# Three moves in the order of VectorE's work: differences of the first set, a left-over product, and the gates' low parts in a hybrid decoder layer

## The chip, the cores and the metric

The kernel runs on one core of a Trainium2 chip. The metric is the device time of one execution in microseconds (us); the kernel before takes 1325.04 us in the median of three runs (1324.93 to 1326.69). Engines are named as in the profile: PE is TensorE's matmuls and PEld its weight loads, DVE is VectorE, ACT is ScalarE, POOL is GpSimd, SP is SyncE, which here issues nearly all DMAs.

## The reference

One decoder layer on 2048 tokens of width 1024, in float32. Cut to what matters:

```python
xn = rms_norm(h, ln_g)
b_gate, c_gate, x_conv, g_conv, x_lru, g_lru = split(xn @ w_in)      # 6 x 1024 columns
y_conv = b_gate * causal_conv3(c_gate * x_conv)                      # group A
u = causal_conv4(x_lru) + conv_b                                     # group B
r = sigmoid(u_per_head @ w_a + b_a); i = sigmoid(u_per_head @ w_i + b_i)
a = exp(8 * r * log_sigmoid(lam))
h_t = a_t * h_(t-1) + sqrt(1 - a_t**2) * (i_t * u_t)                 # scan over the tokens
y = concat(headwise_rms(y_conv) * silu(g_conv), headwise_rms(h) * silu(g_lru))
out = rms_norm(h + y @ w_out)
```

Nearly all arithmetic lies in the two projections, 2048 x 1024 x 6144 and 2048 x 2048 x 1024. The gates r and i are small matmuls, 64 x 64 for each of 16 heads.

## The kernel before

**Precision.** Every float32 operand of a matmul is split into a high part (a cast to fp32r on ACT) and a low part (the value less its high part, a subtraction, mostly on DVE, in the helper at line 163). A product of two split operands is three matmuls: high x high, high x low, low x high. In the profile th and tl are the parts of the moving operand (the tokens' side), s holds both parts of the weights, st both parts of the gates' operand.

**Seven products instead of eight.** A projection step computes two column blocks of 128 for 1024 tokens as a 2 x 2 block product by the Strassen-Winograd scheme: seven products, numbered 0 to 6, on sums and differences of the four blocks of each operand. A product is four blocks of 128 of the inner dimension (j = 0 to 3) times three matmuls, so 12 matmuls into one PSUM accumulator of 128 x 512 (`bank`, five buffers in the pool of the products, two in that of the gates). Products share accumulators: 0, 1 and 2 and 5 go into A, 3 and 6 into B, 4 into C. After product 0 ACT copies A out to q1, after product 1 to u2, after product 2 to rr (lines 1299, 1302, 1305); the next product into A must wait for that copy. The helper `put` then combines accumulators and copies into the four results 11, 12, 21, 22 on DVE.

**Steps, slots, order.** There are 64 steps. Steps 0 to 23 are the input projection of the first 1024 tokens, in rounds of three: l (group B's x and gate), a (c and x of group A), b (its b and gate). Steps 24 to 47 do the same for the second 1024 tokens, 48 to 55 and 56 to 63 the output projection. A step runs its products slot by slot in program order, and the order of all engines' instructions is the program's own (the scheduler is told to keep it). Work behind a product is put off by slots: `at(n, f)` runs f at the n-th following `tick()`, and each slot begins with a tick, which runs what is due in the order in which it was put there. Each engine works its instructions strictly in this order, so an instruction that waits holds up all that stand behind it.

Usually slot 0 runs product 0, slot 1 the sixth product that the step before left over (`pend`: it goes into that step's B), and slots 2 to 6 the products 1, 3, 2, 4, 5; the step's own product 6 is left over again (`ORDER`, lines 1245 to 1318). When the set of tokens or the projection changes, the moving operands change too. The opening step (24, 48, 56) runs eight plain products, and the step after it (25, 49, 57, called late) the order `AFTER`, 0, 4, 5, 1, 3, 2, and leaves product 6 over to the next.

**The first three steps** have no sums and differences of the tokens' blocks yet. They run eight plain half products each, in eight slots (`plain`, lines 1166 to 1177). In their shadow the differences are made: `bit(j)` (line 1140) lists four pieces of work for each j, with six subtractions on DVE and two casts on ACT for each j: b12 - b11 and b22 - b12, then b22 less the first, with the casts and low parts of the operands 2 and 1, and the raw value of operand 6 (`last`). `do_bits(n)` runs the next n of these 16 pieces. The second step (step 1) runs two in each of its eight slots (`after1`), so all of them; the third step (`after2`) casts operands 3 and 6, prepares the weights of step 3 with `prep`, and calls `do_bits(2)` too, which finds nothing left.

**The tokens' change.** Class `Change` makes the operands of the second set, its method `of_x(q)` slot by slot: q is 0 to 7 in step 23, 8 to 15 in step 24, 16 to 21 in step 25. Operand 6 is the last. At q = 21, slot 5 of step 25, `sixth(0, 1)` subtracts, casts and takes the low parts for j = 0 and 1; a tick later, in slot 0 of step 26, `sixth(2, 3)` does so for j = 2 and 3. Slot 1 of step 26 runs the left-over product of step 25, which reads operand 6.

**The gates.** In an l step, `lru` (lines 693 to 799) puts off its work after result 12: the convolution u, then `sth`, which casts u's halves of 64 partitions into the two tiles st[0] and st[1]; a slot later `stl`, two subtractions of 64 x 1024 on DVE for the low parts; two slots on `gates(0)`, four matmuls on the first 512 tokens, two on st[0] and two on st[1] (line 736), then `sigs(0)`, four sigmoids on ACT (line 743) that free the two PSUM buffers; and, two slots after gates(0), `gates(1)` and `sigs(1)` for the other 512 tokens.

Of the kernel before, what the change touches and what calls it, by code (L numbers as in the profile page):

```python
# [12 lines left out]
F32 = mybir.dt.float32  # L13
F32R = mybir.dt.float32r
AF = mybir.ActivationFunctionType
ALU = mybir.AluOpType
# [4 lines left out]
C = 512  # L21
NC = S // C
NB = C // P
# [15 lines left out]
def hymba_kernel(ctx: ExitStack, tc: tile.TileContext, x, xt, w_in, par, lamc, w_gate, w_out, final_g, out):  # L39
# [27 lines left out]
    def piece(name):  # L67
        return rawp.tile([P, C], F32, tag="raw", name=name)
# [75 lines left out]
    def at(slots, *fs):  # L144
        if slots == 0:
            for f in fs:
                f()
        else:
            due.append([slots, fs])
# [12 lines left out]
    def tt(out, a, b, op, eng=None):  # L162
        (eng or nc.vector).tensor_tensor(out=out, in0=a, in1=b, op=op)  # L163
# [99 lines left out]
    def set_of(n):  # L263
        kind, h, _ = steps[n]
        return h + (2 if kind == "o" else 0)

    def opens(n):
        return n > 0 and set_of(n) != set_of(n - 1)
# [153 lines left out]
    class Change:  # L422
# [34 lines left out]
            for i, v in ((2, b11), (3, b12), (1, b22), (6, b21)):  # L457
                self.r[i, j] = v

        def sixth(self, *js):  # L460
            for j in js:
                tt(self.r[6, j], self.r[6, j], self.r[1, j], ALU.subtract)
            self.cut([(6, j) for j in js])

        def of_x(self, q):
            if q == -4:
                for j in range(NB):
                    self.get(5, j, piece("traw"))
            if q == 0:
                self.pair(0)  # L470
                self.pair(1)
            if q == 3:
                for j in range(NB):
                    self.get(4, j, piece("traw"))
                self.pair(2)
                self.pair(3)
            if 9 <= q <= 12:
                self.sums(q - 9)
            if q == 21:
                self.sixth(0, 1)  # L480
                at(1, lambda: self.sixth(2, 3))
            self.cut({1: ((5, 0), (5, 1)), 2: ((5, 2), (5, 3)), 4: ((0, 0), (0, 1)), 5: ((4, 0), (4, 1)),
                      6: ((4, 2), (4, 3)), 7: ((0, 2), (0, 3)), 8: ((7, 0), (7, 1)), 9: ((7, 2), (7, 3)),
                      11: ((1, 0),), 12: ((1, 1),), 13: ((1, 2), (1, 3)), 14: ((3, 0), (3, 1)),
                      17: ((3, 2), (3, 3)), 18: ((2, 0), (2, 1)), 19: ((2, 2), (2, 3))}.get(q, ()))
# [205 lines left out]
    LO, HI = slice(0, 64), slice(64, P)  # L691
    N2 = 2 * C

    def lru(h, k, late=0, early=0):
# [6 lines left out]
        v = {}  # L701
# [20 lines left out]

        def stl():
            st = v["st"]
            for j, (hi, lo) in enumerate(((LO, HI), (HI, LO))):
                tt(st[j][lo], v["u"][hi], st[j][hi].bitcast(F32), ALU.subtract)

        def gates(i):
            sl = slice(i * C, (i + 1) * C)
# [308 lines left out]
    with tc.manual_schedule(engines={ENG.PE, ENG.Activation, ENG.DVE, ENG.Pool, ENG.SP}):  # L1038
# [122 lines left out]
        def do_bits(n):  # L1161
            for f in bits[:n]:
                f()
            del bits[:n]
# [14 lines left out]
        def after1(s):  # L1179
            i = {2: 2, 3: 3, 5: 0, 7: 1}.get(s)  # L1180
            if i is not None:
                s_hi(2, i)
            do_bits(2)
            if i is not None:
                s_lo(2, i)

# [9 lines left out]
        load_next(3)  # L1196

        def after2(s):
            do_bits(2)
            if s in (1, 2, 3, 4, 6, 7):  # L1200
                prep(3, (0, 1, 2, 3, 0, 4, 5)[s - 1])
            if s >= 4:
                j = s - 4
                for i, v in ((3, tr[j][1]), (6, t6[j])):
                    T[i, j] = t_tile(i, j)
                    nc.scalar.copy(T[i, j][0], v)
                for i, v in ((3, tr[j][1]), (6, t6[j])):
                    low(v, T[i, j])
# [7 lines left out]
        for n in range(PLAIN, N):  # L1216
            kind, h, k = steps[n]
            S_ = Sn[n]
            last = n + 1 == N
            new = not last and set_of(n + 1) != set_of(n)  # L1220
            soon = n + 2 < N and set_of(n + 2) != set_of(n + 1)
            put = lru(h, k, 2) if opens(n) and kind == "l" else consumer[kind](h, k)
            if n == 3 * KT + 6:
                work_on[0] = jobs()
            if opens(n):
                cc = {}
                for s, (which, i, t) in enumerate(((12, 1, 5), (22, 3, 5), (11, 1, 4), (21, 3, 4),
                                                   (11, 0, 0), (12, 0, 7), (22, 2, 7), (21, 2, 0))):
                    tick()
                    change.slot(8 + s)  # L1230
                    if s in (0, 3, 4, 6):
                        prep(n + 1, (3, 4, 5, 6)[(0, 3, 4, 6).index(s)])
                    first = which not in cc
                    if first:
                        cc[which] = bank()
                    for j in range(NB):
                        mm(cc[which], S_, T, i, j, first and j == 0, not first and j == NB - 1, k=t)
                    if not first:
                        put(which, cc[which], None)
                    if s == 4:  # L1240
                        load_next(n + 2, 4)
                continue
            late = opens(n - 1)
            bk = {}
            slots = (0, 6) + ORDER[1:] if not late else AFTER
            for s in range(6 if late else 8 if new or last else 7):
                i = slots[s]
                place[0] = {"l": 0, "a": 7, "b": 14}.get(kind, 0) + s
                tick()
                if soon and s == 3:  # L1250
                    T2 = {}
                    change = Change(set_of(n + 2), T2)
                if soon and s > 3:
                    change.slot(s - 8)
                if new:
                    change.slot(s)
                if late:
                    change.slot(16 + s)
                    if s == 0:
                        prep(n, 7)  # L1260
                elif n > 0 and opens(n - 2):
                    if s == 0:
                        prep(n, 5)
                        prep(n, 6)
                    elif s == 2:
                        prep(n, 7)
                elif s == 0:
                    prep(n, 6)
                elif s == 2:
                    prep(n, 7)  # L1270
                if new and s > 0:
                    if s in (1, 3, 4, 5):
                        prep(n + 1, (1, 3, 4, 5).index(s) + 1)
                    elif s > 5:
                        prep(n + 2, s - 5)
                elif s > 0:
                    prep(n + 1, s - 1)
                if s == 3:
                    load_next(n + 2, 3 if late else 4)
                if s == 1 and not late:  # L1280
                    if pend is not None:
                        S6, B, put0, u20 = pend
                        alone = B is None
                        if alone:
                            B = bank()
                        for j in range(NB):
                            mm(B, S6, T, 6, j, alone and j == 0, j == NB - 1, not alone)
                        put0(21, B, u20)
                        pend = None
                    continue  # L1290
                b = {0: "A", 1: "A", 2: "A", 5: "D" if late else "A", 3: "B", 6: "B", 4: "C"}[i]
                first = b not in bk
                if first:
                    bk[b] = bank()
                for j in range(NB):
                    mm(bk[b], S_, T, i, j, first and j == 0, j == NB - 1, not first)
                if i == 0:
                    q1 = sm_q1[0] = sm("q1")
                    nc.scalar.copy(q1, bk["A"])  # L1299
                elif i == 1:  # L1300
                    u2 = sm_u2[0] = sm(("u2", "rr")[n % 2])
                    nc.scalar.copy(u2, bk["A"])  # L1302
                elif i == 2:
                    rr = sm(("rr", "u2")[n % 2])
                    nc.scalar.copy(rr, bk["A"])
                    put(22, bk["B"], rr)
                    if late:
                        put(12, bk["D"], rr)
                elif i == 4:
                    put(11, bk["C"], q1)  # L1310
                elif i == 5 and not late:
                    put(12, bk["A"], None)
                elif i == 6:
                    put(21, bk["B"], u2)
            if new:
                T = T2
            elif not last:
                pend = (S_, bk["B"], put, u2)
# [46 lines left out]
```

## Time and profile before

| what | value |
|---|---|
| median of three runs | 1325.04 us (1324.93 to 1326.69) |
| profiled execution, its own time | 1325.2 us |
| its span in the profile | 1323.4 us |
| mean granted clock of TensorE | 0.997 |
| busy: PE, PEld, DVE, ACT, POOL | 1293.5, 1058.0, 1040.3, 749.1, 245.2 us |
| data moved by DMA | 355.29 MB, 268 GB/s over the span |

The span is the profiled part of that execution, from the first instruction to the last; the time includes what lies around it. A timeline row gives start, duration, engine, line, operation, output<-inputs, shapes and count; the brackets give the idle time of the engine before the row and what ended it. A row of the waits gives the waiting engine and line, who ended the wait, the total in us, how often, and the longest. Matmuls are pipelined: one is shown with about 0.39 us, and the next starts 0.23 us after it. A row with x2 or x3 merges instructions that follow one another, and its duration runs from the first start to the last end. The line 163 is the helper of all two-operand operations, so these are told apart by their tiles.

### The profile page before, as it was taken

How to read it: one execution, taken by the hardware profiler on the slowest of the kernel's cores; microseconds unless marked ns; L12 is line 12 of the kernel's file. 1: busy time of each engine (PE TensorE's matmuls, PEld its weight loads, DVE VectorE, ACT ScalarE, POOL GpSimd, SP SyncE). 2: the span in 40 equal slices, each digit the busy share in tenths (PEclk: the TensorE clock that was granted, in tenths of full speed). 3: DMA queues.
4: the chain of work that ended last, by engine and by line, in shares of the span. 5: the costliest groups of instructions: out<-in, count | busy, mean ns of one | idle time of the engine just before them, and what ended most of it. 6: DMA issues, size and time to landing. Idle time of an engine off the chain costs nothing.

```text
span 1323.4 us, 16676 instructions
## 1 busy us (share of the span) xinstructions
PE 1293.5 (98%) x5688; PEld 1058.0 (80%) x5688; DVE 1040.3 (79%) x1252; ACT 749.1 (57%) x1141; POOL 245.2 (19%) x189
## 2 busy tenths in 40 slices
PE   7989999999999999999999999999999999999997
PEld 6868878787878787878888888888888788887886
DVE  7789898999989897978566676667549777649886
ACT  7576758566675657466554545364457433445453
POOL 3204233344334340002010110101011000000000
PEclk9999999999999999999999999999999999999999
DMA  7138787888989888542789999999779887697654
GB/s 292 32 116 292 279 288 251 299 327 277 339 289 324 294 295 300 195 157 74 247 314 297 333 354 332 338 350 363 237 273 330 267 257 239 235 404 276 231 181 160
DMA packets 157958, 355.29 MB, mean 268 GB/s; under 512 B 16944, under 2 KB 51760, under 8 KB 157872
## 3 DMA queue, kind: packets, MB, share of 16 engines
q1 hardware_dynamic: 153264, 338.17, 73.7%
q0 software_dynamic: 4320, 15.73, 3.1%
q8 instruction: 45, 0.74, 0.2%
q14 instruction: 41, 0.34, 0.1%
q10 hardware_dynamic: 288, 0.32, 0.1%
HBM read 217.11 MB, written 137.04 MB: 268 GB/s over the span
## 4 chain that ended last, share of the span: by engine, by line
PE 55%; DVE 22%; DMA 10%; issue 6%; ACT 6%; SPq 1%; POOL 0%; DVEq 0%; ACTq 0%; POOLq 0%
PE bank L999 53%; DVE s L163 5%; DVE tl L163 2%; DVE u L710 2%; DMA s<-so 2%; PE gate L736 2%; DMA sd<-s 1%; DVE st L163 1%; DVE r L770 1%; DMA raw<-in_w_in_dram 1%; DMA xr<-od 1%; DVE sums L641 1%; DVE traw L163 1%; ACT i L743 1%; ACT r L743 1%
## 5 line engine op out<-in xcount | busy, mean ns | idle before, releaser
L999 PE MATMUL bank<-th,s 128*128 128x512 f32 x3632 | 1130.2, 390 | 9.6 <-ACT rr L1302 2.8
L999 PEld LDWEIGHTS bank<-th,s 128*128 128x128 f32 x3632 | 682.1, 188 | 157.4 <-ACT rr L1302 4.1
L999 PE MATMUL bank<-tl,s 128*128 128x512 f32 x1816 | 707.8, 390 | 1.8 <-DVE tl L163 1.6
L999 PEld LDWEIGHTS bank<-tl,s 128*128 128x128 f32 x1816 | 341.1, 188 | 75.0 <-DVE tl L163 3.4
L163 POOL TENSOR_TENSOR s<-raw,s 128x512 fp32r<-128x512 f32 x62 | 110.6, 1796 | 245.8 <-ACT s L200 207.4
L200 ACT CAST s<-raw 128x512 fp32r<-128x512 f32 x140 | 85.3, 618 | 76.4 <-PE bank L999 45.4
L163 POOL TENSOR_TENSOR gb<-gb,sg 128x1024 f32<-128x1024 f32 x16 | 43.4, 2712 | 336.4 <-ACT sg L669 298.2
L163 DVE TENSOR_TENSOR s<-raw,s 128x512 fp32r<-128x512 f32 (+1 forms) x125 | 93.1, 768 | 10.6 <-ACT s L1058 6.7
L163 DVE TENSOR_TENSOR s<-s,s 128x512 fp32r<-128x512 f32 x105 | 85.5, 814 | 1.9 <-ACT s L200 1.4
L163 DVE TENSOR_TENSOR tl<-traw,th 128x512 fp32r<-128x512 f32 x85 | 60.8, 748 | 23.1 <-ACT th L438 16.9
L200 ACT CAST s<-s 128x512 fp32r<-128x512 f32 x105 | 64.9, 618 | 12.6 <-DVE s L163 12.5
L710 DVE SCALAR_TENSOR_TENSOR u<-xl,pt,u 128x1024 f32<-128x1024 f32 x48 | 61.5, 1280 | 7.8 <-ACT u L706 7.2
L1299 ACT COPY q<-bank 128x512 f32<-128x512 f32 x58 | 34.0, 585 | 54.0 <-PE bank L999 44.4
L820 DVE SCALAR_TENSOR_TENSOR t<-p,pt,t 128x1024 f32<-128x1024 f32 x32 | 46.5, 1454 | 16.6 <-ACT t L817 15.9
L743 ACT ACTIVATE r<-gate,pt 64x512 f32<-64x512 f32 x64 | 43.8, 684 | 17.4 <-PE gate L736 16.6
L1302 ACT COPY rr<-bank 128x512 f32<-128x512 f32 x31 | 18.1, 584 | 55.2 <-PE bank L999 55.2
L163 DVE TENSOR_TENSOR st<-u,st 64x1024 fp32r<-64x1024 f32 x32 | 47.2, 1476 | 1.0
L1302 ACT COPY u<-bank 128x512 f32<-128x512 f32 x27 | 15.8, 585 | 53.4 <-PE bank L999 53.4
L163 DVE TENSOR_TENSOR raw<-raw 128x512 f32<-128x512 f32 x41 | 44.9, 1095 | 0.2
L438 ACT CAST th<-traw 128x512 fp32r<-128x512 f32 x64 | 36.2, 618 | 15.6 <-DVE traw L163 13.9
L743 ACT ACTIVATE i<-gate,pt 64x512 f32<-64x512 f32 x64 | 43.8, 685 | 1.1
L163 DVE TENSOR_TENSOR traw<-traw 128x512 f32<-128x512 f32 x60 | 42.3, 709 | 2.2 <-DMA traw<-in_w_out_dram 1.1
(169 smaller groups left out, 1267.4 us busy)
## 6 DMA issues: line engine op xcount, KB each, us to landing
sd<-s SPq DMA_DIRECT2D x151, 512.0 KB
s<-sd SPq DMA_DIRECT2D x151, 512.0 KB
raw<-in_w_in_dram SPq DMA_DIRECT2D x104, 256.0 KB
raw<-yd SPq DMA_DIRECT2D x64, 256.0 KB
traw<-in_w_out_dram SPq DMA_DIRECT2D x64, 256.0 KB
so<-so SPq DMA_DIRECT2D x22, 512.0 KB
s<-so SPq DMA_DIRECT2D x22, 512.0 KB
yd<-gl SPq DMA_DIRECT2D x32, 256.0 KB
```

The source lines that it names most:

```text
L163: (eng or nc.vector).tensor_tensor(out=out, in0=a, in1=b, op=op)
L200: nc.scalar.copy(dst[i][0], val(i))
L438: nc.scalar.copy(self.dst[i, j][0], self.r[i, j])
L641: nc.vector.tensor_reduce(out=sums[0][:, kt * R:(kt + 1) * R].rearrange("p (q b) -> p q b", q=4), in_=y.rearrange("p (b q a) -> p q b a", ...
L710: nc.vector.scalar_tensor_tensor(out=v["u"], in0=o1[:, 1 + j:1 + j + N2], scalar=lw[j], in1=v["u"], op0=ALU.mult, op1=ALU.add)
L736: nc.tensor.matmul(ps[j], v["gw"][n][:, j, :], v["st"][j][:, sl], start=(n == 0), stop=(n == 1))
L743: nc.scalar.activation(out=g_[hi, sl], in_=v["ps"][j][src], func=AF.Sigmoid, bias=pt[src, bias + k:bias + k + 1])
L770: nc.vector.tensor_tensor_scan(out=r, data0=r, data1=v["u"], initial=init, op0=ALU.mult, op1=ALU.add)
L820: nc.vector.scalar_tensor_tensor(out=tcur["t"], in0=p[:, 2 + j:2 + j + N2], scalar=cw[j], in1=tcur["t"], op0=ALU.mult, op1=ALU.add)
L999: nc.tensor.matmul(bank, a[:, js], b, start=start and n == 0, stop=stop and n == 2, skip_group_check=more)
L1299: nc.scalar.copy(q1, bk["A"])
L1302: nc.scalar.copy(u2, bk["A"])
```

## The change

There are three parts.

1. `stl` is cut by columns: for each half of 512 tokens, the low parts of both st tiles, so four subtractions of 64 x 512 in the order first half of st[0], first half of st[1], second half of st[0], second half of st[1].
2. Slots 6 and 7 of the second step run no pieces of `bit`; the four pieces of j = 3 run in the third step, one in each of slots 0 to 3, ahead of that slot's `prep`.
3. At the tokens' change, `sixth` subtracts for all four j in slot 5 of step 25, and all four casts and low parts follow a tick later. Step 26 runs product 3 in slot 1, the left-over product in slot 2 and product 1 in slot 3; products 2, 4 and 5 keep their slots. No other step fits the condition.

```diff
-        def sixth(self, *js):
-            for j in js:
+        def sixth(self):
+            for j in range(NB):
                 tt(self.r[6, j], self.r[6, j], self.r[1, j], ALU.subtract)
-            self.cut([(6, j) for j in js])
+            at(1, lambda: self.cut([(6, j) for j in range(NB)]))
...
             if q == 21:
-                self.sixth(0, 1)
-                at(1, lambda: self.sixth(2, 3))
+                self.sixth()
...
         def stl():
             st = v["st"]
-            for j, (hi, lo) in enumerate(((LO, HI), (HI, LO))):
-                tt(st[j][lo], v["u"][hi], st[j][hi].bitcast(F32), ALU.subtract)
+            for i in range(2):
+                sl = slice(i * C, (i + 1) * C)
+                for j, (hi, lo) in enumerate(((LO, HI), (HI, LO))):
+                    tt(st[j][lo, sl], v["u"][hi, sl], st[j][hi, sl].bitcast(F32), ALU.subtract)
...
-            do_bits(2)
+            if s < 6:
+                do_bits(2)
...
         def after2(s):
-            do_bits(2)
+            do_bits(1)
...
             slots = (0, 6) + ORDER[1:] if not late else AFTER
+            if kind != "o" and n > 1 and opens(n - 2):
+                slots = (0, 3, 6, 1, 2, 4, 5)
...
-                if s == 1 and not late:
+                if i == 6 and not late and s < 3:
```

## The prediction

> **What bounds the kernel now.** I read the page first, then who waits for whom on TensorE, then a table by stretches, then the timelines of the places that the diff touches.
>
> ```profile
> span 1323.4 us, 16676 instructions
> PE 1293.5 (98%) x5688; PEld 1058.0 (80%) x5688; DVE 1040.3 (79%) x1252; ACT 749.1 (57%) x1141; POOL 245.2 (19%) x189
> ...
> PE gate L736 <- ACT i L743: 3.8, 9, 2.0
> ...
> PE gate L736 <- DVE st L163: 2.4, 8, 0.6
> ...
> 76.78:80.17 3.39, 2.89 (x8) 1.92 (x7) 1.38 (x2) 3.34 (x7) 0.00 (x0) 0.50 0.02 5
> ...
> 82.80:127.10 44.30, 43.57 (x193) 35.73 (x192) 42.57 (x47) 31.85 (x48) 12.56 (x9) 1.00 0.74 262
> ...
> 254.30:314.60 60.30, 59.80 (x261) 48.55 (x260) 56.50 (x58) 38.70 (x56) 23.60 (x15) 1.00 0.87 307
> ```
>
> TensorE is busy 98% of the span, so time is won only where it stands still: at the gates' matmuls (the two waits quoted from the list) and at a few products. In the first set VectorE is nearly as full: 56.50 us of a 60.30 us round of three steps, and 42.57 of 44.30 just after the plain steps. There TensorE's gains can be taken back by VectorE. The columns of a stretch are its length, then the busy time of PE, PEld, DVE, ACT and POOL, the granted clock, DMA share and GB/s; for 3.39 us, right behind the longest of these waits, the clock was 0.50.
>
> Idle time counts from the modelled end of a matmul. I use starts instead: undisturbed matmuls start 0.23 us apart, a product of 12 takes 2.72.
>
> **Part 1, the gates' low parts by halves.** Two 64x1024 subtractions become four 64x512, the two first halves ahead. A 64x512 is not in the trace. Below, half of a 64x1024 (2.47 for two at 65.64, under part 2, so 0.62); above, a half beside POOL, 3.45/4 = 0.86 (at 190.60). I take 0.69, the 128x512 rows of the same columns, plus the 0.03 that stands between two of them: 4 x 0.72 = 2.88 against 2.50 with the 0.03 behind, so 0.38 us more VectorE in each of 16 steps. The first gates' matmuls then wait for 1.44 us of subtractions, not 2.50. One round:
>
> ```profile
> PE gate L736 <- DVE st L163: 1.4, 6, 0.2
> ...
> 193.59 0.39 PE L736 MATMUL gate<-st,bl 128*128 128x512 f32 x1
> 194.20 0.47 PE L736 MATMUL gate<-st,bh 128*128 128x512 f32 x1 [0.23 <-DVE st L163]
> ...
> 190.60 3.45 DVE L163 TENSOR_TENSOR st<-u,st 64x1024 fp32r<-64x1024 f32 x2
> ...
> 191.57 1.40 POOL L163 TENSOR_TENSOR s<-raw,s 128x512 fp32r<-128x512 f32 x1 [2.15 <-ACT s L200]
> ```
>
> The second pair starts 0.61 us after the matmul before it instead of 0.23, and the pipe refills for 0.08 more: 0.46 lost. With halves its operand is there at 190.60 + 1.44 = 192.0, or 193.4 if the POOL instruction comes between; it is wanted at 193.8. The first row is the waits of 190 to 510 us: six such rounds, 6 x 0.46 = 2.8 us. The next wait, of the second half's gates for ACT's sigmoids, stays: those follow a copy of a product of the same TensorE stream and move with it. VectorE's 0.38 lies in its 3.8 us of room per round (60.30 - 56.50). The second set gives nothing: six waits here and the two of the first step are all eight of the list.
>
> **Part 2, four differences of block 3 into the third step.** They leave slots 6 and 7 of the second step (six VectorE instructions, two ACT casts) and go to slots 0 to 3 of the third. No DMA moves.
>
> ```profile
> 65.64 2.47 DVE L163 TENSOR_TENSOR st<-u,st 64x1024 fp32r<-64x1024 f32 x2
> ...
> 71.76 2.14 DVE L163 TENSOR_TENSOR traw<-traw 128x512 f32<-128x512 f32 x3
> ...
> 75.02 0.69 DVE L163 TENSOR_TENSOR tl<-traw,th 128x512 fp32r<-128x512 f32 x1
> ...
> 78.92 1.28 DVE L820 SCALAR_TENSOR_TENSOR t<-p,pt,t 128x1024 f32<-128x1024 f32 x1 [2.01 <-ACT t L817]
> ...
> 72.48 0.62 ACT L1145 CAST th<-traw 128x512 fp32r<-128x512 f32 x1 [2.02 <-DVE traw L163]
> 73.01 0.62 ACT L1058 CAST s<-raw 128x512 fp32r<-128x512 f32 x1
> 73.94 0.62 ACT L1145 CAST th<-traw 128x512 fp32r<-128x512 f32 x1 [0.31 <-DVE traw L163]
> ...
> 74.94 0.68 ACT L743 ACTIVATE r<-gate,pt 64x512 f32<-64x512 f32 x1
> ...
> 67.01 0.47 PE L736 MATMUL gate<-st,bh 128*128 128x512 f32 x1 [0.61 <-DVE st L163]
> ...
> 68.74 0.40 PE L999 MATMUL bank<-th,s 128*128 128x512 f32 x1
> ...
> 76.37 0.50 PE L736 MATMUL gate<-st,bh 128*128 128x512 f32 x1 [2.01 <-ACT i L743]
> ...
> 78.79 0.63 PE L999 MATMUL bank<-th,s 128*128 128x512 f32 x1
> ```
>
> This is the longest stall of the list. The gates at 76.37 wait for sigmoids that begin at 74.94, behind two casts of block 3 that wait for VectorE. Take out both waits (2.02, 0.31) and both casts (about 0.52 each to the next start) and add the 0.38 of part 1: sigmoids from 74.94 - 3.37 + 0.38 = 71.95, the first pair of accumulators free 1.4 later, the second at 74.75. TensorE comes earlier too: halves are ready at 66.3 and 67.05, so the first gates end and the next product starts near 67.7 (68.74 before), and two products later it is 73.2. The second gate pair starts at 74.75 and the product behind it near 75.3 instead of 78.79: 3.5 us, and some 0.7 more if the half clock goes.
>
> VectorE has the six instructions (3.95 us, 71.76 to 75.71) still to do. It ends the second step near 73.5 (76.91 before), must wait for ACT to about 75.9 (the row at 78.92, with one difference done meanwhile), and then works through. What it meets next:
>
> ```profile
> 126.54 2.85 POOL L163 TENSOR_TENSOR gl<-gl,sg 128x1024 f32<-128x1024 f32 x1
> ...
> 128.17 0.69 DVE L163 TENSOR_TENSOR xx<-bank,rr 128x512 f32<-128x512 f32 x1 [1.04 <-ACT rr L1305]
> 128.89 3.91 DVE L163 TENSOR_TENSOR st<-u,st 64x1024 fp32r<-64x1024 f32 x2
> ...
> 133.50 0.39 PE L999 MATMUL bank<-th,s 128*128 128x512 f32 x1
> ```
>
> Before, it stood still 2.0 us at 78.92, 1.7 in the stretch from 82.80 to 127.10 (44.30 - 42.57) and 1.0 at 128.17. Afterwards: start 3.4 earlier, 4.0 more work, 0.3 less idle at 78.92, and of the 1.7 what waited for TensorE falls away. If none of it does, VectorE is 0.3 later at 127, if all does, 1.4 earlier; I take 0.9 earlier, since a late VectorE finds its products done. It no longer waits at 128.17 and begins the next gates' low parts at 126.9 instead of 128.9. Held up by POOL's multiplication as far as 128.5, the two first halves end near 129.8, and the product that started at 133.50 starts at 130.45. So of 4.2 us, **3.05** reach the rounds; this holds the first round's gate wait too.
>
> [...]
>
> **Part 3, the left-over product a slot later.** Step 26 runs product 3 in slot 1 and the left-over sixth product of step 25 in slot 2; all four differences come first, all casts and low parts a tick later.
>
> ```profile
> 562.67 0.40 PE L736 MATMUL gate<-st,bl 128*128 128x512 f32 x1
> 564.96 0.50 PE L999 MATMUL bank<-th,s 128*128 128x512 f32 x1 [1.89 <-DVE xx L163]
> ...
> 576.19 0.71 PE L614 MATMUL norm_ps<-rt,sel 128*96 128x256 f32 x4 [0.82 <-ACT i L743]
> 576.74 0.39 PE L999 MATMUL bank<-th,s 128*128 128x512 f32 x1
> ...
> 558.00 2.47 DVE L163 TENSOR_TENSOR st<-u,st 64x1024 fp32r<-64x1024 f32 x2
> ...
> 566.79 1.29 DVE L163 TENSOR_TENSOR tl<-traw,th 128x512 fp32r<-128x512 f32 x2
> ...
> 573.24 1.15 ACT L817 ACTIVATE t<-p,pt 128x1024 f32<-128x1024 f32 x1 [2.08 <-DVE p L163]
> 574.30 0.57 ACT L1302 COPY u<-bank 128x512 f32<-128x512 f32 x1
> ...
> 551.29 11.21 SPq L226 DMA_DIRECT2D s<-sd  x5
> ...
> 99.42 0.50 PE L999 MATMUL bank<-th,s 128*128 128x512 f32 x1 [0.73 <-ACT q L1299]
> ```
>
> Now the left-over product waits 2.1 us for its accumulator (read by xx) and 1.1 inside for its operands. Product 3 can start at 562.9: its weights' load was issued at 551.29, 11 us earlier. It covers 2.72 us, to 565.65. VectorE runs the gates' low parts (2.9 from 558.00), a multiplication of 1024 columns (1.2, as one of the st row) and the four differences (2.5) to 564.5, then xx to 565.1, the four low parts 565.65 to 568.1, one per 0.60 against 0.68 that the product needs: it waits about 0.5 for the first. So TensorE is at 569.0 with one product more done: 2.6 won. Two things follow. The wait for the sums of norms (0.8 idle at 576.19, 1.0 from start to start) goes, since the sigmoids before it come 2 us earlier. But products 1 and 2, which share an accumulator, become neighbours: product 2 must wait for the copy at 574.30. The cheapest such wait is at 99.42, 0.9 from start to start, with ACT idle; here four sigmoids and the 1.15 convolution stand ahead of the copy, 569.7 + 2.8 + 1.15 + 0.6 = 574.2. So the product of 576.74 starts at 574.2: **2.5** won (3.5 if the copy were free, 0.5 if 2 us more stand ahead of it). No DMA is added; a weight tile is freed by another product of the same slots.
>
> **Sum.** 3.05 + 2.8 + 2.5 = 8.35, from the profiled execution's 1325.2 (span 1323.4, 1.8 around it; the median of the runs is 0.2 lower, which I leave out): **1316.8 us**.
>
> **Rivals.**
> - VectorE takes all of part 2 back. For it: 42.57 busy of 44.30, and 4 us pushed in there. Against: 4 us of idle to absorb them. 1316.8 + 3.05 = 1319.9.
> - The copy of product 1 eats part 3: 1316.8 + 2.5 = 1319.3. For it: the ACT row at 573.24. Against: ACT waited 2.08 there.
> - A POOL instruction gets between the halves in every round, and the rounds keep their wait: 1316.8 + 2.8 = 1319.6. For it: POOL's row at 191.57, inside the low parts. Against: wanted at 193.8, ready at 193.4 even so.
> - VectorE does not cap part 2: 4.2 instead of 3.05, 1315.7.
> - Slower: the diff's cut does nothing because waits are set for whole tiles, so the first gates wait for all four pieces. Then each of eight gates loses 0.8 more than now (the first pair waits too, and 0.38 longer), the first one 0.9: +7.3; part 2 keeps 2, part 3 its 2.5, so 1328. It decides if halves of one tile are not told apart. Against it:
>
> ```profile
> 1318.71 0.72 ACT L987 ACTIVATE ob<-ob,sq 128x512 f32<-128x512 f32 x1 [0.23 <-DVE sq L954]
> 1318.71 0.75 DVE L961 SCALAR_TENSOR_TENSOR ob<-ob,sq,fg 128x512 f32<-128x512 f32 x1
> ```
>
> There two engines write the halves of one ob tile at the same time.
>
> **How the numbers follow.** Forecast 0.49; the rivals in their order 0.13, 0.12, 0.07, 0.04, 0.06; two or more of the first three at once, 1322 to 1325, 0.09. About 0.2% (2.65 us) is what a measurement of this kernel tells from no change. Faster: 0.49 + 0.13 + 0.12 + 0.07 + 0.04 = 0.85; same: 0.09 and a sixth of the slower case, 0.10; slower 0.05. Low end: no cap (1.15) and the full part 3 (1.0), 1314.6, and 1.0 for what I put too late in VectorE's and ACT's order, 1313.6; high end: two rivals together, 1322.4. Beyond it lie most of the 0.09 and the slower case.
>
> **What would show it.** The gates' second pair 0.23 after the first in the rounds; no half clock near 77; the third step's last product 4 us earlier than before but the next gates only 3; six low parts or differences between 562 and 568 without TensorE idle over 0.6; a wait of about 1 us on ACT u or rr L1302 in step 26. Wrong: gates waiting for the last of four pieces, or TensorE idle over 2 us between 80 and 130.

## The result and the profile after

The changed kernel takes **1317.95 us** in the median of six runs (1316.72 to 1319.67), the kernel before on the same chip 1326.56 (six runs, 1324.93 to 1329.05). The two medians lie 8.6 us apart. The ratio on record, 0.9939 with a 95% interval of 0.9929 to 0.995, makes it 8.1 us won, between 6.6 and 9.4; below, 8.1 is used. Forecast were 1316.8 us and a gain of 8.35. The profiled execution is the slowest of the six, 1319.67 us, with a span of 1317.9 against 1323.4; so the ledger below explains 5.5 us, and what this one execution lacks is part of the story. Line numbers shift in the changed kernel, mostly by one to four: gates L737, sigmoids L744, products L1000, sums of norms L613, the copies of products 0, 1, 2 L1303, L1306, L1309; where only one part is carried they lie a line or two elsewhere. The copies of products 1 and 2 swap the names u and rr from step to step, so they are told apart by their lines.

First the page and the list of waits on TensorE:

```profile
span 1317.9 us, 16708 instructions
PE 1293.0 (98%) x5688; PEld 1060.1 (80%) x5688; DVE 1043.3 (79%) x1284; ACT 748.4 (57%) x1141; POOL 245.8 (19%) x189
...
PE bank L1000 <- ACT u L1309: 2.5, 2, 1.8
...
PE gate L737 <- ACT i L744: 1.9, 8, 0.7
...
PE bank L1000 <- DMA s<-sd: 0.9, 1, 0.9
```

The wait of the gates for st (2.4 us, eight times) is no longer in the list, and the gates' longest wait for sigmoids fell from 2.0 to 0.7. New at the top is a product that waits 1.8 us for ACT's copy u at L1309, the copy of product 2, and there is one new wait for a weights' DMA. VectorE has 32 instructions more, one for each subtraction that was cut, and 3.0 us.

The stretches of the table by time, the first two where the half clock was and where one is now, then the two shown of before (columns as there):

```profile
76.78:80.17 3.39, 3.39 (x17) 2.81 (x16) 3.26 (x5) 3.30 (x6) 0.10 (x1) 1.00 0.00 0
109.84:113.24 3.40, 3.40 (x10) 2.65 (x9) 3.40 (x4) 0.44 (x1) 2.02 (x1) 0.50 1.02 416
82.80:127.10 44.30, 41.63 (x175) 33.59 (x175) 42.30 (x47) 31.29 (x47) 15.08 (x9) 0.96 0.76 274
254.30:314.60 60.30, 60.06 (x264) 48.99 (x263) 57.23 (x61) 38.66 (x56) 23.77 (x15) 1.00 0.88 308
```

In the round (last row) TensorE gained 0.26 us of busy time and VectorE 0.73. In the stretch from 82.80 to 127.10 TensorE lost: 41.63 us of 44.30 against 43.57, at a granted clock of 0.96, and GpSimd was busy for 15.08 us against 12.56. Where that happens, in TensorE's timeline:

```profile
75.35 0.39 PE L1000 MATMUL bank<-th,s 128*128 128x512 f32 x1
...
106.23 0.39 PE L1000 MATMUL bank<-th,s 128*128 128x512 f32 x1
108.44 0.50 PE L1000 MATMUL bank<-th,s 128*128 128x512 f32 x1 [1.82 <-ACT u L1309]
...
110.43 0.63 PE L1000 MATMUL bank<-tl,s 128*128 128x512 f32 x1
110.86 1.06 PE L1000 MATMUL bank<-th,s 128*128 128x512 f32 x2
...
132.91 0.39 PE L1000 MATMUL bank<-th,s 128*128 128x512 f32 x1
```

The product behind the second gates starts at 75.35 (78.79 before). Product 5 of the fourth step (step 3, the first with seven products) then waits for the copy of product 2, starts 2.21 us after the matmul before it instead of 0.23, and its matmuls from 110 on are 0.43 apart: half clock. The product behind the next gates starts at 132.91, against 133.50. In the kernel before, product 5 waited for nothing; it is the second of the two matmuls of this row and starts at 110.45:

```profile
110.23 0.61 PE L999 MATMUL bank<-th,s 128*128 128x512 f32 x2
```

Found by counting matmuls from the gates, the lead over the kernel before is 4.12 us at the last product of the third step (88.97 for 93.09), 2.01 at product 5 and 0.59 behind the next gates: 2.0 go to this wait, and the 1.4 behind product 5 to the half clock (from there to the product behind the gates it takes 24.47 us, before 23.05).

The whole span as a ledger, by starts on TensorE (us):

| from the start to | before | after | won in this part |
|---|---|---|---|
| product behind the first step's second gates | 78.79 | 75.35 | 3.44 |
| first gates of round 1 | 132.22 | 131.99 | -3.21 |
| first gates of round 7 | 495.60 | 492.69 | 2.68 |
| gates of step 26 | 561.99 | 558.59 | 0.49 |
| product 2 of step 26 | 576.74 | 570.77 | 2.57 |
| end of the span | 1323.4 | 1317.9 | -0.47 |

The last part holds the new DMA wait, at 725.34.

### The profile page after: what moved, and what is told of

The parts are those of the page before. It is cut to its first block, busy times and chain, and to the rows that moved or that the text cites. A ratio compares the mean times of both kernels' runs of the same rounds, so it can differ in the third digit from the quotient of the medians.

```text
span 1317.9 us, 16708 instructions
## 1 busy us (share of the span) xinstructions
PE 1293.0 (98%) x5688; PEld 1060.1 (80%) x5688; DVE 1043.3 (79%) x1284; ACT 748.4 (57%) x1141; POOL 245.8 (19%) x189
## 4 chain that ended last, share of the span: by engine, by line
PE 69%; DVE 9%; DMA 7%; ACT 5%; issue 3%; SPq 0%; POOL 0%; DVEq 0%; ACTq 0%; POOLq 0%
PE bank L1000 68%; DMA s<-so 2%; DVE tl L163 2%; PE gate L737 2%; DVE s L163 1%; DMA sd<-s 1%; ACT i L744 1%; DVE r L771 1%; ACT r L744 1%; DVE traw L163 1%; DMA tl<-td 1%; DMA traw<-in_w_out_dram 1%; DMA zr<-rsd 1%; DMA fg<-in_final_g_dram 1%; DVE u L163 1%
## 5 line engine op out<-in xcount | busy, mean ns | idle before, releaser
L1000 PE MATMUL bank<-th,s 128*128 128x512 f32 x3632 | 1131.3, 390 | 10.6 <-ACT u L1309 2.5
L1000 PEld LDWEIGHTS bank<-th,s 128*128 128x128 f32 x3632 | 682.4, 188 | 159.1 <-ACT u L1309 4.5
L1000 PE MATMUL bank<-tl,s 128*128 128x512 f32 x1816 | 708.3, 390 | 1.9 <-DVE tl L163 1.7
L1000 PEld LDWEIGHTS bank<-tl,s 128*128 128x128 f32 x1816 | 341.3, 188 | 74.9 <-DVE tl L163 3.6
L1303 ACT COPY q<-bank 128x512 f32<-128x512 f32 x58 | 33.9, 585 | 47.5 <-PE bank L1000 37.8
L744 ACT ACTIVATE r<-gate,pt 64x512 f32<-64x512 f32 x64 | 43.7, 683 | 18.1 <-PE gate L737 17.2
L163 DVE TENSOR_TENSOR st<-u,st 64x512 fp32r<-64x512 f32 x64 | 51.6, 807 | 2.0
L1306 ACT COPY rr<-bank 128x512 f32<-128x512 f32 x31 | 18.1, 584 | 55.0 <-PE bank L1000 55.0
L1306 ACT COPY u<-bank 128x512 f32<-128x512 f32 x27 | 15.8, 585 | 53.8 <-PE bank L1000 53.8
L744 ACT ACTIVATE i<-gate,pt 64x512 f32<-64x512 f32 x64 | 43.7, 684 | 1.1
```

The source lines that it names most:

```text
L744: nc.scalar.activation(out=g_[hi, sl], in_=v["ps"][j][src], func=AF.Sigmoid, bias=pt[src, bias + k:bias + k + 1])
L1000: nc.tensor.matmul(bank, a[:, js], b, start=start and n == 0, stop=stop and n == 2, skip_group_check=more)
```

## The experiments

Each ran beside the kernel before on its chip, so ratios are compared; the median of before was 1325.67 us for the first four, 1325.96 for the next four and 1326.11 for the last.

**The three parts alone.** The first carries only the cut of `stl`, the second only the moved pieces of j = 3, the third only `sixth` and the order of step 26; the hunks are those of the diff above. Some texts put on record before the runs count the steps otherwise: their "product 5 of the third step" is that of step 3, the fourth, and the gate multiplication of their "second step" that of step 2, the third.

> Only part 1, the gates' low parts by halves. My theory: in the rounds of the first set the second gate pair follows the first by 0.23 us instead of 0.61, seven times, so the last gates of that set (495.6 before) start 2.8 us earlier, and the time falls by 2.8 (ratio about 0.998). In the first step the gates' second half waits for sigmoids, and these come 0.4 later, not earlier, so nothing is won there. Rival: GpSimd's instruction gets between the halves, the pairs keep their 0.6 and the time stays within 0.5 us.

> Only part 2, four pieces of block 3's differences in the third step. My theory after seeing the trace of the changed kernel: the stall of 2.0 us before the second gates of the first step goes and the product behind them starts about 3.4 us earlier (78.8 before), but VectorE and with it ScalarE are late in step 3, and product 5 of that step waits about 2 us for the copy of product 2 near 108; net 0.5 to 2 us faster at the next gates, more or less 1.7 for where the half clock falls. Rival, as in my prediction's sum: nothing waits until the next gates and 3 us are kept. Second rival: all of it is given back, 0.

> Only part 3, the left-over product a slot later with all differences first. My theory: from the start of the gates in slot 1 of step 26 to the start of product 2 it takes 12.2 us instead of 14.75, with about 1 us of waiting for the copy of product 1 left, and the time falls by 2.5. Rival: the gain shown in the changed kernel hangs on parts 1 and 2 (VectorE in time), alone it is under 1 us.

| part alone | median us | ratio to before | 95% interval |
|---|---|---|---|
| halves | 1323.71 | 0.999 | 0.9981 to 0.9998 |
| pieces of j = 3 | 1323.25 | 0.998 | 0.997 to 0.9991 |
| tokens' change | 1322.25 | 0.9975 | 0.9965 to 0.9985 |
| all three | 1317.95 | 0.9939 | 0.9929 to 0.995 |

The three ratios multiply to 0.9945, inside the interval of the whole: within the noise the parts add. With the halves alone the rounds 1 to 7 take 360.58 us by the first gates (135.35 to 495.93) against 363.38: 2.80 less, the forecast term. But only some 1.3 us of it arrive in the time (0.3 to 2.5 by the interval). Part of the loss is at the second gates of the first step. Their row with the halves alone:

```profile
78.37 0.80 PE L738 MATMUL gate<-st,bh 128*128 128x512 f32 x1 [3.42 <-ACT i L745]
```

They wait 3.42 us instead of 2.01. Counted from the last matmul ahead of the first gates (67.62, before 66.01), TensorE is there 1.02 us sooner, and the sigmoids let it go 0.39 later, as expected. The half clock behind this wait lasts 6.8 us (77.79 to 84.61) instead of 3.41, and the first gates of round 1 come 1.52 us later by the same count. This profile has two more half clocks, at 16.35 and 565.89, so one execution does not settle how much is lost where. In the whole change part 2 takes this wait away, and rounds 1 to 7 win 2.68. The pieces alone already show the new wait ahead of product 5 of the fourth step:

```profile
107.78 0.50 PE L999 MATMUL bank<-th,s 128*128 128x512 f32 x1 [1.54 <-ACT u L1306]
```

No half clock followed it there (from it to the product behind the next gates it takes 23.43 us, in the changed kernel 24.47), and that product came at 131.21: 2.29 us won, a little over the 0.5 to 2 expected and short of the rival's 3. The tokens' change alone brings product 2 of step 26 to 11.81 us behind the gates (563.64 to 575.45) against 14.75: 2.94 won.

**Product 1 and product 2 no longer neighbours.** The changed kernel with one more product between product 1 and its successor in the same accumulator.

```diff
-                slots = (0, 3, 6, 1, 2, 4, 5)
+                slots = (0, 3, 1, 6, 2, 4, 5)
...
-                if i == 6 and not late and s < 3:
+                if i == 6 and not late and s < 4:
```

> The changed kernel with the left-over product one slot later still, order 0, 3, 1, left-over, 2, 4, 5, so that products 1 and 2 are no neighbours. My theory: the wait for the copy of product 1 (0.84 idle, 1.1 with the pipe's refill) and the wait for the first low part (0.46) both go, 1.5 us less than the changed kernel at product 2. Rival: the left-over result comes a slot later, so the convolution that uses it is late and holds VectorE, and the 1.5 come back within the next steps.

1317.35 us (1316.14 to 1318.89), ratio 0.9939 (0.9927 to 0.9951), the same as the whole change within its interval. In TensorE's timeline:

```profile
567.50 0.39 PE L1000 MATMUL bank<-th,s 128*128 128x512 f32 x1
...
611.86 0.50 PE L1000 MATMUL bank<-th,s 128*128 128x512 f32 x1 [0.65 <-ACT rr L1309]
```

Product 2 starts with no wait, 10.72 us behind the gates (556.78) against 12.18: the copy's price is 1.46 us. But a product at 611.86 now waits for a copy, and the gates behind it come 57.95 us after those of step 26 against 58.56 in the changed kernel. Of 1.46 us, 0.6 are left: more than half comes back in the next steps, as the rival had it; that it does so by a late convolution on VectorE is not shown.

**The gate multiplication on VectorE.** Why is the copy of product 2 in the fourth step late? These are the rows of VectorE, ACT and GpSimd in the changed kernel:

```profile
97.40 2.28 DVE L771 TENSOR_TENSOR_SCAN r<-r,u 128x1024 f32<-128x1024 f32 x1
...
101.78 2.89 DVE L163 TENSOR_TENSOR s<-raw 128x512 f32<-128x512 f32 x1
...
105.43 0.62 ACT L200 CAST s<-s 128x512 fp32r<-128x512 f32 x1 [2.48 <-DVE s L163]
...
107.81 0.58 ACT L1309 COPY u<-bank 128x512 f32<-128x512 f32 x1
...
100.74 3.38 POOL L163 TENSOR_TENSOR gb<-gb,sg 128x1024 f32<-128x1024 f32 x1
```

And the same work in the kernel before:

```profile
98.65 2.28 DVE L770 TENSOR_TENSOR_SCAN r<-r,u 128x1024 f32<-128x1024 f32 x1
...
104.61 2.89 DVE L163 TENSOR_TENSOR s<-raw,s 128x512 fp32r<-128x512 f32 x1
...
104.72 0.62 ACT L200 CAST s<-s 128x512 fp32r<-128x512 f32 x1 [0.51 <-DVE s L163]
...
108.79 0.62 ACT L200 CAST s<-raw 128x512 fp32r<-128x512 f32 x1 [2.39 <-PE bank L999]
109.31 0.58 ACT L1305 COPY u<-bank 128x512 f32<-128x512 f32 x1
...
104.10 2.85 POOL L163 TENSOR_TENSOR gb<-gb,sg 128x1024 f32<-128x1024 f32 x1
```

In both, a VectorE subtraction that takes 0.69 us at most wherever no GpSimd row lies beside it takes 2.89 while GpSimd multiplies. Before, it was one on which ACT's cast did not wait, and ACT then stood idle for 2.39 us, waiting for TensorE. With the change GpSimd's multiplication comes 3.4 us earlier (100.74 for 104.10), VectorE's scan only 1.25 (97.40 for 98.65), so the multiplication now falls on the subtraction ahead of the cast's own; the cast begins at 105.43, and the copy, behind a square of 1024 columns and another cast, at 107.81. That the 2.89 us are the cause was tried by taking this one multiplication off GpSimd (it belongs to the gate of the third step, step 2, and is put off into the fourth):

```diff
-                silu(g)
+                silu(g, 0, nc.vector if h == 0 and k == 0 else None)
```

> The changed kernel, but in the first set's second step (the one around 78 to 108 us) the gate multiplication of its first tile goes to VectorE instead of GpSimd. Theory: ScalarE copies product 2 of the third step late because a rounding it has in front waits for VectorE, and VectorE is held for 2.89 us at 101.78 beside GpSimd's multiplication of 3.38 us. Then the spacing of 2.20 us ahead of product 5 of that step (108.44 us) falls to about 0.4, the half clock that follows it has no stall to follow, and the median comes 1.5 to 3 us under the changed kernel's 1317.95: 1315 to 1316.5. Rival: VectorE is simply full until then; the multiplication costs it another 1.2 us, the wait ahead of product 5 stays at 1.5 to 2.5 us or moves to the gates after it, and the median stays within 1 us of 1318.

**1315.47 us** (1314.85 to 1317.41), ratio 0.9921 (0.9907 to 0.9935). Rows of VectorE, ACT and TensorE:

```profile
101.94 0.68 DVE L163 TENSOR_TENSOR s<-raw 128x512 f32<-128x512 f32 x1
...
105.07 1.22 DVE L163 TENSOR_TENSOR gb<-gb,sg 128x1024 f32<-128x1024 f32 x1
...
103.38 0.62 ACT L200 CAST s<-s 128x512 fp32r<-128x512 f32 x1 [0.27 <-DVE s L163]
...
105.76 0.58 ACT L1309 COPY u<-bank 128x512 f32<-128x512 f32 x1
...
106.39 0.62 PE L1000 MATMUL bank<-th,s 128*128 128x512 f32 x2
...
129.38 0.39 PE L1000 MATMUL bank<-th,s 128*128 128x512 f32 x1
```

The subtraction is back at 0.68, the cast 2.05 us earlier, the copy too, and product 5 follows product 4 without a break (the second of the two matmuls at 106.39 is its first). The product behind the next gates starts at 129.38, 4.12 us before the 133.50 of the kernel before. The expectation held, wait, half clock and time. The changed kernel itself did not run beside this one, and the two intervals overlap (from 0.9929 to 0.9935); on the same chip the order by tiles below, which still waits at product 5, took 1317.69.

**The same edit in the kernel before**, without any of the three parts:

> The kernel before, none of the three parts, with only the gate multiplication of the first tile of the first set's second step on VectorE instead of GpSimd. Theory (that multiplication costs time only once part 2 has brought the products forward by 3.5 us, so that the copy of product 2 is needed sooner): in the kernel before product 5 of the third step starts at 110.45 with no wait and no stall stands ahead of the next gates at 132.22, so nothing is to be won: the product behind these gates stays within 0.5 us of 133.50 and the median within 1 us of the kernel before. Rival (GpSimd's multiplication costs time of its own, whatever stands around it): the median falls by 1.5 to 3 us, as it did from 1317.95 to 1315.47 in the changed kernel.

1325.61 us against 1326.11, ratio 0.9998 (0.9989 to 1.0007): nothing. Product 5 had no wait to lose. So the multiplication on GpSimd is no cost of its own; part 2 made it one. The product behind the next gates came 0.95 earlier than in the profile of before, outside the half microsecond that was expected; this profile has no half clock near 77, the other has.

```profile
132.55 0.39 PE L999 MATMUL bank<-th,s 128*128 128x512 f32 x1
```

**Both edits together**, the order with product 1 apart and the multiplication on VectorE:

> Two edits together: the order of step 26 in which the copy of product 1 has another product in front of it (1317.35 us by itself) and the gate multiplication on VectorE. If the late copy of product 2 in the third step is VectorE's block beside GpSimd, the two add: 1317.35 less 1.5 to 3 us, 1314.3 to 1315.9. Rival (VectorE is simply full): 1316.7 to 1318.5.

1315.27 us (1314.9 to 1320.29), ratio 0.9926 (0.9911 to 0.9941): inside the expected range, but not to be told from the multiplication alone. In its profile product 5 does not wait either (product 4 from 106.02, product 5 from 108.74). The multiplication alone is the simpler of the two, and both medians lie below the changed kernel's.

**Two pieces moved instead of four**, to see whether the start at 75.35 is worth anything with the wait at 108 behind it:

```diff
-            if s < 6:
+            if s < 7:
                 do_bits(2)
```

> The changed kernel with two of the four bit pieces left in the first set's second step and two moved to its third (before: none moved; changed: all four). Theory (what is won early in the step is capped by VectorE and the copies of the next step): the product behind the second gates starts later than the 75.35 us of the changed kernel, by 0.8 to 1.8 us, but product 5 of the third step starts within 0.4 us of 108.44 and its wait is 0.8 to 1.8 us shorter; the median stays within 0.7 us of 1317.95. Rival (each piece moved is worth its share of TensorE's time, no cap): the delay of 0.8 to 1.8 us goes through to product 5 and to the next gates, and the median is 1318.7 to 1319.8.

1320.02 us (1319.09 to 1321.09), ratio 0.9954 (0.9941 to 0.9968). TensorE's rows, and ACT's copy:

```profile
75.99 0.80 PE L737 MATMUL gate<-st,bh 128*128 128x512 f32 x1 [2.50 <-ACT i L744]
...
78.41 0.63 PE L1000 MATMUL bank<-th,s 128*128 128x512 f32 x1
...
134.07 0.39 PE L1000 MATMUL bank<-th,s 128*128 128x512 f32 x1
...
109.71 0.62 ACT L200 CAST s<-raw 128x512 fp32r<-128x512 f32 x1 [2.39 <-PE bank L1000]
```

Neither theory had it. The product came 3.06 us later, not 0.8 to 1.8, so two pieces put back bring the whole stall of the second gates back. The wait ahead of product 5 is gone, as the row of ACT, idle for TensorE again, shows, and yet product 5 starts 2.95 us later (111.39), not within 0.4 as the cap would have it. Behind the next gates 1.16 are left (134.07 for 132.91), but of the 1.79 between, some 1.5 are the changed kernel's own half clock (last section). This profile holds half clock too, from 75.81 to 82.63, and the median is 2.1 us above the changed kernel's, just beyond the rival's range. No cap is shown here, and its absence is not either.

**Halves in the order of the tiles**, both of st[0] ahead of both of st[1]:

```diff
-            for i in range(2):
-                sl = slice(i * C, (i + 1) * C)
-                for j, (hi, lo) in enumerate(((LO, HI), (HI, LO))):
+            for j, (hi, lo) in enumerate(((LO, HI), (HI, LO))):
+                for i in range(2):
+                    sl = slice(i * C, (i + 1) * C)
```

> The changed kernel with the four halves of the low parts in the order of the tiles: both halves of the first tile, then both of the second. The work is the same, only the order differs. Theory (the rounds won 2.80 us because the second pair of gates finds its operand, the second piece, sooner): its operand is now the third piece, 0.71 us later, and the second pair's spacing rises from 0.23 to 0.5 to 0.95 us in each of the seven rounds: 2 to 5 us lost from the first gates of these rounds to the last, median 1320 to 1323. Rival (the halves win because smaller pieces cost VectorE less or because the first pair of gates starts sooner): spacing 0.23 to 0.3, rounds as long as in the changed kernel, median within 0.7 us of 1317.95.

1317.69 us (1316.47 to 1321.04), ratio 0.994 (0.9926 to 0.9954): no loss, my theory of the order is wrong. The rows of VectorE, GpSimd and TensorE in one round, first of the changed kernel:

```profile
190.01 3.82 DVE L163 TENSOR_TENSOR st<-u,st 64x512 fp32r<-64x512 f32 x4
...
190.96 1.61 POOL L163 TENSOR_TENSOR s<-raw,s 128x512 fp32r<-128x512 f32 x1 [2.12 <-ACT s L200]
...
192.97 0.39 PE L737 MATMUL gate<-st,bl 128*128 128x512 f32 x1
193.19 0.39 PE L737 MATMUL gate<-st,bh 128*128 128x512 f32 x1
```

and of this one, with the tiles' order:

```profile
188.10 3.59 DVE L163 TENSOR_TENSOR st<-u,st 64x512 fp32r<-64x512 f32 x4
...
191.06 0.39 PE L737 MATMUL gate<-st,bl 128*128 128x512 f32 x1
191.28 0.41 PE L737 MATMUL gate<-st,bh 128*128 128x512 f32 x1
```

The four pieces end at 191.69 here; the last takes about 0.7, so the third is done near 191.0, ahead of the second pair at 191.28, which follows after 0.22. In the changed kernel they end at 193.83, 0.64 after the second pair has begun. What wins is that the gates do not wait for the last piece; in which order the first three come makes no difference here.

## Why the prediction was right, and where it was not

**Part 1, 2.8 us: right.** Rounds 1 to 7 won 2.68 (2.80 alone), the second pair follows after 0.22, and VectorE pays 0.37 more in the round shown (3.82 for 3.45; forecast 0.38). GpSimd does come between the pieces, as the rival had it (its row at 190.96; the four take 3.82 us where four of 0.69 and their gaps make 2.88), and the gates do not wait even so. The slower case, waits per whole tile, is excluded by the gates that begin while the last piece runs. Not weighed was that the halves alone lengthen the first step's stall; the whole change hides it.

**Part 2, 3.05 us: the stall right, the cap wrong.** The sigmoids were forecast from 71.95, the product behind the second gates at 75.3; it came at 75.35, the half clock at 77 went, and the sigmoids' row is this:

```profile
71.93 0.69 ACT L744 ACTIVATE r<-gate,pt 64x512 f32<-64x512 f32 x1
```

The step that failed is the one that puts VectorE's cap at the next gates' low parts ("It no longer waits at 128.17 and begins the next gates' low parts at 126.9"). It still waits there, longer than before, in the changed kernel:

```profile
127.36 0.69 DVE L163 TENSOR_TENSOR xx<-bank,rr 128x512 f32<-128x512 f32 x1 [1.49 <-ACT rr L1309]
128.08 3.96 DVE L163 TENSOR_TENSOR st<-u,st 64x512 fp32r<-64x512 f32 x4
```

and also with the multiplication on VectorE, where 4.12 of the forecast 4.2 us came through:

```profile
125.09 0.69 DVE L163 TENSOR_TENSOR xx<-bank,rr 128x512 f32<-128x512 f32 x1 [1.03 <-ACT rr L1309]
```

So at these gates VectorE follows TensorE and caps nothing. It was free at 125.87 (the row's start less its wait), 1.26 us earlier than before, so its load was forecast well; what it waits for was not. The cap sat 20 us earlier, in the chain from GpSimd's multiplication by VectorE's subtraction and ACT's cast to the copy of product 2. The forecast counted VectorE's load over the stretch; it did not ask which instruction GpSimd would meet once it ran ahead of VectorE. In the kernel before, two low parts took 3.45 us beside a GpSimd row (at 190.60) and 2.47 without one (at 65.64), and I weighed that as a rival against the halves of part 1 alone. In the changed kernel a subtraction took 2.89 us for 0.69 beside a multiplication of 3.38, and that decided in part 2. The size was near all the same, and that is luck in part. Where no half clock follows the wait, 2.29 (the pieces alone) and 2.52 (the order by tiles: 130.98 for 133.50) arrive, forecast 3.05; in the profiled execution it is 0.59, the half clock having cost some 1.5 more. About 0.95 of these gains goes with the half clock near 77 that the profile of before happens to have: against the 132.55 of the kernel before with the multiplication on VectorE, which has none there, they are 1.34 and 1.57. My own sign of error, TensorE idle over 2 us between 80 and 130, came within 0.2 of its bound. Of the signs that would show the forecast right, the third held only in its first half: the third step's last product came 4.12 us earlier, but the next gates 0.23 in the profiled execution, not 3.

**Part 3, 2.5 us: right**, 2.57 measured, and by its terms:

```profile
562.95 0.50 PE L1000 MATMUL bank<-tl,s 128*128 128x512 f32 x1 [0.30 <-DVE tl L163]
...
569.29 0.64 PE L613 MATMUL norm_ps<-rt,sel 128*96 128x256 f32 x4
570.77 0.50 PE L1000 MATMUL bank<-th,s 128*128 128x512 f32 x1 [0.84 <-ACT u L1306]
...
570.15 0.56 ACT L1306 COPY u<-bank 128x512 f32<-128x512 f32 x1
```

The left-over product waits 0.30 for a low part (forecast about 0.5), the norms wait for nothing, and product 2 waits for the copy behind the sigmoids and the convolution, as forecast.

**The sum.** 8.35 was forecast, 8.1 measured. With part 2 as it comes where no half clock follows the wait, 2.4 + 2.68 + 2.57, and 0.49 between round 7 and step 26 that the forecast did not have (the second pair of round 7 among it), it is 8.1 too, without the 0.47 that this execution loses in the last part. The time came out right with one term 0.6 too large and another 0.5 left out; that these two cancel is luck.

## What to carry to other kernels

When a change pulls work forward, compare how far each engine comes forward at the next stage: an engine that gains more than its neighbour (here GpSimd by 3.4 us, VectorE by 1.25) meets other instructions of it, and a block that was harmless (here 2.89 us) can land in front of a copy that TensorE needs (here a wait of 1.82). Count the load of an engine over a stretch only after following the chain to each accumulator's release. Cut an operand so that a consumer needs not wait for the last piece; the order of the earlier pieces may not matter (here the gates' second pair came 0.22 us after the first in either order, 0.61 before).

## What the runs showed of the hardware that was not expected

**Half clock followed nine stretches of 3.41 us, each with 1.82 to 2.84 us of idle time.** The periods of half clock in the middle of the span are 3.41 us long (76.77 to 80.18 in the kernel before, 109.83 to 113.25 in the changed one), or twice that (77.79 to 84.61 with the halves alone). By the recorded clock half clock begins at 76.77 and at 1319.22 in the kernel before, 364 times 3.413 us apart, and at 109.83 and 1314.74 in the changed kernel, 353 times. The changed kernel fell into one after a stall of 1.82 us, the kernel with the halves by tiles did not after one of 1.80. Take a grid of 3.41 us, laid from the recorded change of clock in each of the eleven profiles (before, changed, nine experiments), and add up TensorE's idle time, by the modelled ends, in each cell. Leaving out the end of the span, the nine cells with 1.82 to 2.84 us of it were all followed by half clock (2.01 from 73.35 to 76.77 in the kernel before, 1.82 from 106.42 to 109.83 in the changed one). Of those below, up to 1.81 us, only three were, at the very start (cells between 12.9 and 17.5 us, with 1.44 to 1.56 us), besides two cells inside a half clock that went on. At the start of the span, then, the idle time alone does not decide. The stall of 1.80 us lay across a cell's border, 1.44 on one side. These rows of that kernel, one of TensorE's timeline and one of the table by stretches, show the full clock behind it:

```profile
108.01 0.50 PE L1000 MATMUL bank<-th,s 128*128 128x512 f32 x1 [1.80 <-ACT u L1309]
...
108.02:111.42 3.40, 3.40 (x15) 2.81 (x16) 3.40 (x4) 1.31 (x3) 2.34 (x1) 1.00 1.04 424
```

From product 5 of the fourth step to the product behind the next gates it takes 22.97 us (108.01 to 130.98), the changed kernel 24.47 (108.44 to 132.91): here one half clock cost 1.5 us, nearly a fifth of what the change won. Where the grid lies against the program differs from execution to execution (76.77 and 109.83 are 9.69 cells apart), so one stall of some 2 us costs 2 or 3.5, an estimate from these numbers. That this makes most of the spread of 3 to 6 us between runs of one kernel is argued, not shown: time and mean granted clock go together in the 26 runs of the kernel before beside the first four experiments (correlation -0.70), hardly in the 11 beside the next four (-0.22).
